# Two unused tiles that shift where the SBUF tiles of a two-block transformer kernel begin

## The chip, the cores and the metric

The kernel runs on one core of one Trainium2 chip. The metric is device time in microseconds. The kernel before took 1284.35 us (median of 3 runs, 1283.81 to 1284.84).

## The reference, cut to what matters

Two transformer blocks over 256 tokens of width 1024, all in float32. What matters here is that nearly all of the work is matrix products with weights that are read once from memory:

```
h = rms_norm(x, norm_mix);  proj = h @ w_in            # 5888 columns
att = window attention, ret = chunkwise retention of pieces of proj
merged = sigmoid(ga) * (att @ w_att_o) + sigmoid(gr) * (ret @ w_ret_o)
x = x + merged @ w_out
x = x + (silu(h @ w_gate) * (h @ w_up)) @ w_down        # 2816 hidden
x = rms_norm(x, final_norm)
proj = rms_norm(x) @ w_in_2                             # second block
x = x + concat(gated, chunk attention) @ w_out_2
# PEER: 16384 experts, 16 kept per head and token, 8 heads
q = x @ w_query;  scores = q . sub_keys;  top 16, 16x16 candidates, top 16
out[t] = sum over kept experts e of  g[t,e] * gelu(u_e . x_t) * v_e
```

The expert layer is computed densely: all 16384 rows of u against all tokens (the first layer), a table S of gates times gelu, and S against all rows of v (the second layer).

## The kernel before, in words

Activations are kept transposed, 128 partitions by (block of 128 features, 256 tokens). Every float32 operand of a large product is split in two parts of type float32r: a rounded high part (`hi`, ScalarE, line 95 or 156) and the rest (`lo`, VectorE, line 96 or 157). A product is then three matmuls that add up in PSUM: high by high, high by low, low by high (`mm3`, lines 108 to 112). The trace shows these operands as f32.

`unit` (lines 77 to 100) fetches one block of weights, 128 partitions by 1024 floats, from memory into a buffer `raw` and splits it into `whi` and `wlo`. There are four `raw` buffers and two pools of three pairs `whi`, `wlo`, one of which (`wa`) is closed before the expert layer. A scheduler orders the instructions of each engine; the loads of weights are put 80 places ahead of their uses.

There are three forms of float32r matmul, and a matmul has two operands: the moving one (`rhs`), whose columns stream through TensorE, and the stationary one (`lhsT`), which a weight load (PEld) brings in before each matmul:

- `gemm_t` and `gemm_k` (lines 117 to 129; also written out for `w_att_o`): moving 256 columns of activations (`acth`, `actl`, `hidh`, `hidl`, `att`, `xbh`, `xbl`), stationary 128 columns of `whi` or `wlo`. This is called the 256-column form here.
- `gemm_n` (lines 139 to 151): moving 512 columns of `whi` or `wlo`, stationary 128 columns of activations (`acth`, `actl`).
- `second_layer` (lines 1082 to 1088, matmul on line 1087): moving 512 columns of `whi` or `wlo` (the last six only 256), stationary 128 columns of `keys` or `q`, which hold the split S.

```
109  mm = self.nc.tensor.matmul
110  mm(ps, lhsT=left[0], rhs=right[0], start=first, stop=False)
111  mm(ps, lhsT=left[0], rhs=right[1], start=False, stop=False)
112  mm(ps, lhsT=left[1], rhs=right[0], start=False, stop=last)
```

Besides these there are some 400 plain float32 matmuls (attention, retention, transposes, sums by a column of ones on line 190, expert scores on line 906) and 256 of float16 (line 960).

SBUF is given out from two ends of each partition. Pools that are opened in the ordinary way stack up from the low addresses: `const`, `tiny`, then `xb`, `actp` (the activations), `res`, `work` and what the blocks open. Pools that are opened under `using_default_side("right")` stack down from the high addresses: first `wb` with its four `raw` and three `whi`, `wlo`, then `wa`, and in the expert layer `gs`, `query` (with `keys` and `q`) and others in its place.

Of the kernel before, what the change touches and what calls it, by code (L numbers as in the profile page):

```python
# [7 lines left out]
F32 = mybir.dt.float32  # L8
# [35 lines left out]
class Net:  # L44
# [175 lines left out]
    def run(self):  # L220
        self.wpools, self.turn = [], 0
        with self.tc.using_default_side("right"):
            self.weights("wb", self.stack, 4, 3)
        self.xbp = self.pool("xb", 1)
        with ExitStack() as st:
            actp = self.pool("actp", 2, st)
            self.res = self.pool("res", 2, st)
            self.work = self.pool("work", 2, st)
            with ExitStack() as sw:
                with self.tc.using_default_side("right"):  # L230
                    self.weights("wa", sw, 0, 3)
                x2, h, acc, acg = self.block1(actp)
                x3, h, acc = self.block2(actp, x2, h, acc, acg)
            self.wpools.pop()
            self.peer(st, x3, h, acc)
# [971 lines left out]
```

## Time and profile before

| | |
|---|---|
| median of 3 runs | 1284.35 us |
| the profiled execution's own time | 1283.83 us |
| its span, first to last instruction | 1282.0 us |
| PE busy | 1272.5 us, 99% |
| weight loads busy | 1183.7 us, 92% |
| VectorE busy | 904.6 us, 71% |
| ScalarE busy | 718.3 us, 56% |
| GpSimd busy | 269.9 us, 21% |
| mean granted TensorE clock | 0.999 of full |
| memory read and written | 240.93 and 10.55 MB |

How to read it: the span is 1.8 us shorter than the time of the execution that it belongs to, and that execution is 0.5 us below the median of the runs. A matmul's "busy" time is longer than its share of the engine, since matmuls overlap; what a matmul costs is the distance from its start to the start of the next, called its pitch here. It is read from the starts in the timeline, or from a count in a stretch in which PE is busy all the time.

### The profile page before, as it was taken

To read this page: it belongs to the slowest core of one execution; us is meant where nothing else is said; L and a number is where in the kernel's file an instruction comes from. 1 tells how busy PE (TensorE), PEld (TensorE's weight loads), DVE (VectorE), ACT (ScalarE), POOL (GpSimd) and SP (SyncE) were. 2 spreads that over 40 slices of the span, in tenths; PEclk is the share of its full clock that TensorE was granted. 3 is DMA by queue.
4 is the path that set the end of the run, shared out by engine and by line. 5 is a ranking of instruction groups with operands and counts; after the bars stand their busy time and mean duration, and the time that the engine had idled before them with its cause. 6 is when DMAs were issued, how large, how long until landed. Compare 5 with 4: busy or idle time off the path is not lost.

```text
span 1282.0 us, 23578 instructions
## 1 busy us (share of the span) xinstructions
PE 1272.5 (99%) x9128; PEld 1183.7 (92%) x9128; DVE 904.6 (71%) x1786; ACT 718.3 (56%) x1158; POOL 269.9 (21%) x173
## 2 busy tenths in 40 slices
PE   8999999999999999999999999999999999999998
PEld 8978999999999889999999999999988888888887
DVE  7867577766666877988895566676566666666665
ACT  5555455554454776655554676666455555555553
POOL 2000000000000000008777787773000000000000
PEclk9999999999999999999999999999999999999999
DMA  7735659966666445567777777777767777777764
GB/s 242 267 132 164 181 181 319 320 185 189 173 188 224 149 137 156 178 186 192 180 165 212 182 167 172 175 166 178 216 212 219 219 220 218 217 218 219 218 198 160
DMA packets 91072, 253.02 MB, mean 197 GB/s; under 512 B 26960, under 2 KB 29008, under 8 KB 90832
## 3 DMA queue, kind: packets, MB, share of 16 engines
q1 hardware_dynamic: 68960, 241.58, 61.6%
q0 software_dynamic: 20992, 8.46, 5.9%
q8 instruction: 71, 1.16, 0.4%
q10 hardware_dynamic: 1008, 1.47, 0.3%
q14 instruction: 41, 0.34, 0.1%
HBM read 240.93 MB, written 10.55 MB: 196 GB/s over the span
## 4 chain that ended last, share of the span: by engine, by line
PE 93%; DVE 5%; issue 1%; DMA 0%; ACT 0%; SPq 0%; DVEq 0%; ACTq 0%
PE ax L1087 27%; PE mm L110 21%; PE mm L111 20%; PE mm L112 20%; DVE wlo L96 2%; PE ax L960 1%; DVE itop L759 1%; PE ax L906 0%; DMA xT<-in_xT_dram 0%; DVE stop L757 0%; DVE sc L762 0%; DVE pos L759 0%; ACT whi L95 0%; PE ax L450 0%; PE ax L696 0%
## 5 line engine op out<-in xcount | busy, mean ns | idle before, releaser
L96 DVE TENSOR_TENSOR wlo<-raw,whi 128x1024 fp32r<-128x1024 f32 (+2 forms) x433 | 524.3, 1213 | 236.4 <-ACT whi L95 229.9
L95 ACT ACTIVATE whi<-raw 128x1024 fp32r<-128x1024 f32 (+3 forms) x439 | 457.8, 1045 | 314.4 <-PE mm L111 219.8
L110 PE MATMUL mm<-xbh,whi 128*128 128x256 f32 x1104 | 311.8, 282 | 0.0
L112 PE MATMUL mm<-xbh,wlo 128*128 128x256 f32 x1104 | 308.4, 279 | 0.3 <-DVE wlo L96 0.2
L111 PE MATMUL mm<-xbl,whi 128*128 128x256 f32 x1104 | 308.2, 279 | 0.2 <-DVE xbl L157 0.2
L850 POOL DMA_INDIRECT cmat<-best,pos x128 | 242.0, 1890 | 229.0 <-DVE itop L759 169.6
L110 PE MATMUL mm<-acth,whi 128*128 128x256 f32 x840 | 236.4, 282 | 1.9 <-ACT acth L254 0.8
L111 PE MATMUL mm<-actl,whi 128*128 128x256 f32 x840 | 235.1, 280 | 2.0 <-DVE actl L255 2.0
L112 PE MATMUL mm<-acth,wlo 128*128 128x256 f32 x840 | 234.2, 279 | 0.0
L112 PEld LDWEIGHTS mm<-xbh,wlo 128*128 128x128 f32 x1104 | 207.4, 188 | 1.3 <-DVE wlo L96 0.9
L111 PEld LDWEIGHTS mm<-xbl,whi 128*128 128x128 f32 x1104 | 207.6, 188 | 0.4 <-DVE xbl L157 0.4
L110 PEld LDWEIGHTS mm<-xbh,whi 128*128 128x128 f32 x1104 | 207.6, 188 | 0.2 <-ACT xbh L156 0.2
L110 PEld LDWEIGHTS mm<-acth,whi 128*128 128x128 f32 x840 | 157.8, 188 | 3.2 <-ACT acth L254 1.0
L111 PEld LDWEIGHTS mm<-actl,whi 128*128 128x128 f32 x840 | 157.9, 188 | 2.6 <-DVE actl L255 2.6
L1087 PE MATMUL ax<-whi,q 128*128 128x512 f32 x513 | 158.2, 389 | 0.0
L1087 PE MATMUL ax<-whi,keys 128*128 128x512 f32 x513 | 158.1, 389 | 0.0
L112 PEld LDWEIGHTS mm<-acth,wlo 128*128 128x128 f32 x840 | 157.9, 188 | 0.2 <-DVE wlo L96 0.2
L1087 PE MATMUL ax<-wlo,keys 128*128 128x512 f32 x513 | 158.0, 389 | 0.0
L156 ACT ACTIVATE keys<-S 128x256 fp32r<-128x256 f32 x128 | 53.4, 418 | 151.4 <-PE ax L1087 151.4
L1087 PEld LDWEIGHTS ax<-whi,q 128*128 128x128 f32 x513 | 96.3, 188 | 19.9
L1087 PEld LDWEIGHTS ax<-wlo,keys 128*128 128x128 f32 x513 | 96.3, 188 | 19.9
L1087 PEld LDWEIGHTS ax<-whi,keys 128*128 128x128 f32 x513 | 96.2, 188 | 20.0
(283 smaller groups left out, 1414.2 us busy)
## 6 DMA issues: line engine op xcount, KB each, us to landing
raw<-in_peer_u_dram SPq DMA_DIRECT2D x128, 512.0 KB
raw<-in_peer_v_dram SPq DMA_DIRECT2D x128, 512.0 KB
raw<-in_w_in_b_dram SPq DMA_DIRECT2D x32, 512.0 KB
raw<-in_w_in_a_dram SPq DMA_DIRECT2D x31, 512.0 KB
raw<-in_w_gate_dram SPq DMA_DIRECT2D x22, 512.0 KB
raw<-in_w_up_dram SPq DMA_DIRECT2D x22, 512.0 KB
raw<-in_w_out_dram SPq DMA_DIRECT2D x16, 512.0 KB
cmat<-zero SPq DMA_DIRECT2D x16, 512.0 KB
```

The source lines that it names most:

```text
L95: self.last_copy = nc.scalar.activation(hi[:, s], raw[:, s], AF.Copy).ins
L96: low = (engine or nc.vector).tensor_tensor(out=lo[:, s], in0=raw[:, s], in1=hi[:, s].bitcast(F32), op=OP.subtract)
L110: mm(ps, lhsT=left[0], rhs=right[0], start=first, stop=False)
L111: mm(ps, lhsT=left[0], rhs=right[1], start=False, stop=False)
L112: mm(ps, lhsT=left[1], rhs=right[0], start=False, stop=last)
L156: nc.scalar.activation(hi, src, AF.Copy)
L759: yield cost + 50, lambda: nc.vector.max_index(where[:, o:o + 8], top[:, o:o + 8], vals)
L850: i = nc.gpsimd.indirect_dma_start(self.cmat, bass.IndirectOffsetOnAxis(ap=ps[:, hd, 1, k:k + 1], axis=0), bs[:, hd, 1, k:k + 1], None, co ...
L960: nc.tensor.matmul(C[:, t * 128:t * 128 + 128], lhsT=A[:, t], rhs=G[i][:, t], start=i == 0, stop=i == 1)
L1087: nc.tensor.matmul(banks[tb][o // 512][:, o % 512:o % 512 + e - o], lhsT=s[left][:, ts], rhs=w[right][:, o:e], start=first, stop=end and e ...
```

## The change

A tile of 120 floats (480 bytes in each partition) is taken from the right side before the weights' pool, and a tile of 64 floats (256 bytes) from the left side before the pool `xb`. Nothing reads or writes them.

```
@@ -220,7 +220,9 @@
     def run(self):
         self.wpools, self.turn = [], 0
         with self.tc.using_default_side("right"):
+            self.pool("edge", 1).tile([128, 120], F32, name="edge")
             self.weights("wb", self.stack, 4, 3)
+        self.pool("gap", 1).tile([128, 64], F32, name="gap")
         self.xbp = self.pool("xb", 1)
         with ExitStack() as st:
```

Everything on the right thereby begins 480 bytes lower, and everything on the left from `xb` on 256 bytes higher. The rows of all five engines, with their waits, are the same in the same order as before; only addresses differ. Where the operands of the float32r matmuls begin, as the remainder of the address by 512 bytes (all blocks of one tile lie multiples of 512 bytes apart, so that each kind of operand has one remainder):

| form, matmuls | moving, before | stationary, before | both, after |
|---|---|---|---|
| 256-column form, 6528 | 256 | 480 | 0 |
| `gemm_n`, 512 columns, 384 | 480 | 256 | 0 |
| `second_layer`, 1533 of 512 columns and 6 of 256 | 480 | 480 | 0 |

Of the plain float32 matmuls, the stationary operand of line 190 goes from 256 to 0 and its moving one stays at 384; both operands of line 906 go from 480 to 0; both operands of the matmul on line 510 from 256 to 0. The `raw` buffers go from 480 to 0, `xT` and S from 256 to 0.

## Rows read from the trace of the kernel before

**Rows 1.** The page: busy time of the engines; the chain that ended last by engine

```profile
PE 1272.5 (99%) x9128; PEld 1183.7 (92%) x9128; DVE 904.6 (71%) x1786; ACT 718.3 (56%) x1158; POOL 269.9 (21%) x173
...
PE 93%; DVE 5%; issue 1%; DMA 0%; ACT 0%; SPq 0%; DVEq 0%; ACTq 0%
```

**Rows 2.** Waits of PE, longest and shortest of seven (us in total, times, longest)

```profile
PE mm L111 <- DVE actl L255: 2.0, 3, 0.8
...
PE mm L111 <- DVE xbl L157: 0.2, 1, 0.2
```

**Rows 3.** The chain that ended last, in order of time (start us, us, what)

```profile
3.06 5.13 DMA xT<-in_xT_dram
...
929.79 347.51 PE ax L1087 x1533
```

**Rows 4.** Groups of matmuls by form: line 110's, a third of each kind

```profile
L110 PE MATMUL mm<-xbh,whi 128*128 128x256 f32 x1104 | 311.8, 282 | 0.0
...
L110 PE MATMUL mm<-acth,whi 128*128 128x256 f32 x840 | 236.4, 282 | 1.9 <-ACT acth L254 0.8 <-DVE qkv L294 0.6 <-ACT whi L95 0.5
...
L110 PE MATMUL mm<-whi,acth 128*128 128x512 f32 x128 | 51.4, 401 | 0.0
...
L110 PE MATMUL mm<-hidh,whi 128*128 128x256 f32 x176 | 49.5, 281 | 0.0
...
L110 PE MATMUL mm<-att,whi 128*128 128x256 f32 x32 | 8.9, 279 | 0.0
...
L110 PE MATMUL ax<-acth,whi 128*128 128x256 f32 x24 | 6.9, 287 | 0.0
```

**Rows 5.** Two stretches: length, busy (x count) by engine, granted clock, DMA

```profile
200.00:300.00 100.00, 100.00 (x854) 100.00 (x853) 72.60 (x112) 54.55 (x85) 0.00 (x0) 1.00 0.80 268
300.00:400.00 100.00, 100.00 (x851) 100.00 (x850) 64.46 (x88) 50.45 (x75) 0.00 (x0) 1.00 0.63 185
```

**Rows 6.** Timeline of PE in `gemm_n`, first and last of eight (start us, us)

```profile
420.55 0.40 PE L111 MATMUL mm<-wlo,acth 128*128 128x512 f32 x1
...
422.18 0.40 PE L112 MATMUL mm<-whi,actl 128*128 128x512 f32 x1
```

**Rows 7.** Timeline of PE, second layer: first of six into two banks, and the next

```profile
1273.73 0.39 PE L1087 MATMUL ax<-whi,keys 128*128 128x512 f32 x1
...
1275.09 0.62 PE L1087 MATMUL ax<-whi,keys 128*128 128x512 f32 x2
```

**Rows 8.** Timeline of PE, the last five matmuls of the second layer: first, last

```profile
1277.24 0.28 PE L1087 MATMUL ax<-wlo,keys 128*128 128x256 f32 x1
...
1277.72 0.28 PE L1087 MATMUL ax<-whi,q 128*128 128x256 f32 x1
```

**Rows 9.** Timeline of PE in the retention, plain float32, 256 columns

```profile
86.08 0.59 PE L510 MATMUL ax<-rv,sr 128*128 128x256 f32 x2
86.51 0.59 PE L511 MATMUL ax<-rv,sr 128*128 128x256 f32 x2
```

**Rows 10.** Plain float32 matmuls with little streaming: lines 190 and 906, timeline and durations

```profile
414.89 0.58 PE L190 MATMUL ax<-ones,acg 128*128 128x1 f32 x4
...
L190 PE MATMUL ax<-ones,acg x4: 250/250/250, 414.9 to 415.2; 128*128 128x1 f32 x4
...
511.19 1.05 PE L906 MATMUL ax<-keys,qT 128*128 128x128 f32 x8
...
L906 PE MATMUL ax<-keys,qT 128*128 128x128 f32 x64 | 8.8, 275 | 0.0
```

**Rows 11.** Timeline of PE, 256-column form: ends of 26 pitches and of 18

```profile
154.40 0.28 PE L110 MATMUL mm<-acth,whi 128*128 128x256 f32 x1
...
157.43 0.28 PE L112 MATMUL mm<-acth,wlo 128*128 128x256 f32 x1
...
299.79 0.28 PE L110 MATMUL mm<-acth,whi 128*128 128x256 f32 x1
...
301.91 0.28 PE L110 MATMUL mm<-acth,whi 128*128 128x256 f32 x1
```

More of the change, by code (lines that the diff above doesn't have):

```diff
@@ L222, in run @@
         with self.tc.using_default_side("right"):
+            self.pool("edge", 1).tile([128, 120], F32, name="edge")
             self.weights("wb", self.stack, 4, 3)
+        self.pool("gap", 1).tile([128, 64], F32, name="gap")
         self.xbp = self.pool("xb", 1)
```

## The prediction

> **What bounds the kernel now.** I read the page first: TensorE is busy 99% of the span and the chain that ended last is 93% matmuls, 5% VectorE [rows 1]. Next the waits of PE: seven kinds, the longest 2.0 us in all [rows 2]. Nothing but TensorE's own pace sets the time from the first weights on. The clock is no part of it: the granted clock stands at 1.00 in both stretches that I use, the full level of 2.4 GHz [rows 5]. So everything hangs on the pitch, the distance from one matmul's start to the next's, and on whether an address can change it. The reader is to see three pitches:
>
> - 256-column form (moving 256, stationary 480, as remainders by 512): 854 and 851 matmuls in 100 us each, with PE busy throughout [rows 5]: 200,000 ns / 1705 = 117.3 ns.
> - `gemm_n` (480 and 256): seven pitches from 420.55 to 422.18 [rows 6]: 232.9 ns.
> - second layer (480 and 480): 347.51 us for 1533 matmuls, without a break on the chain [rows 3]: 226.7 ns.
>
> The last two differ in nothing that streams: 512 columns of the same weight tiles at the same remainder, one weight load each. Still they are 6.2 ns apart. I looked for causes other than addresses. One is PSUM: the second layer mostly alternates between two banks, `gemm_n` stays in one. But at its end the second layer also puts three in a row into one bank, twice, and these six take 1275.09 - 1273.73 = 1.36 us, 226.7 ns each [rows 7]. What is left of what I can see is where the stationary operand begins: 480 against 256. So I take it that operand addresses matter when float32r streams at full rate. That is inferred, not isolated: the neighbouring engines' work differs too.
>
> **The change part by part.** It adds no instruction and no wait, and moves none on any queue; the loads, splits and evictions cost what they did. The one load on the chain is that of `xT`, 5.13 us at the start [rows 3]; its target goes from 256 to 0, and no row shows what a target's address does to a transfer; I give it nothing, and a tenth of it either way, 0.5 us, would be lost in the measurement. All other transfers are covered by the loads that run ahead (PE's waits above); the DMA engines are busy 0.63 to 0.80 of the two stretches [rows 5], so a faster PE has room to be fed, and VectorE at 64 to 73% and ScalarE near 55% there too.
>
> What is left are three terms, one per form, and their bounds from below come from the nearest rows, though none of them streams float32r:
>
> 1. The 512-column forms. A plain float32 matmul of 256 columns takes (86.51 - 86.08)/2 = 215 ns [rows 9], to within the rounding of two starts, some 2 ns; I take 216. It streams at half the columns per time, so this is as long as 512 float32r columns at full rate (512/2.4 = 213.3 ns) would take with hardly anything around it. Floor: 216 ns. `gemm_n` stands 16.9 above it, the second layer 10.7.
> 2. The 256-column form. By streaming alone its floor would be half of that, but each matmul needs its weight load, and that has a pace of its own: the one-column matmuls of line 190 start (0.58 - 0.25)/3 = 110 ns apart, the 128-column ones of line 906 (1.05 - 0.275)/7 = 111 ns [rows 10]. Their stationary operands begin at 256 and at 480, so a weight load alone does not mind where it begins; I take 111 ns as the floor. The form stands 6.3 above it.
>
> If alignment took away all that lies above the floors: 6528 x 6.3 = 41.1 us (the counts of line 110's rows, 1104 + 840 + 176 + 32 + 24 = 2176, times three lines [rows 4]), 1533 x 10.7 = 16.4, and 3 x 128 = 384 of `gemm_n` x 16.9 = 6.5. Together 64 us, so 1283.8 - 64 = 1220 us. That is the lower end. The Trainium skill, "TensorE: Matmul & The Clock Gate", section "Back-to-back issue gap", gives N/2.4 + 2.5 ns for an isolated warm stream, 109.2 and 215.8 ns here; by that page the sum would be 76 us and the time 1208; the trace shows no float32r matmul at that pace.
>
> The other end of each term is a loss; it is the second rival below. Between them I take the share that the trace has shown for one step in addresses: going from 480/256 to 480/480 is worth 6.2 of 16.9 ns above the floor, 0.37. The change brings both operands to the start of a 512-byte block, which I count as one more such step for every form: `gemm_n`'s pitch then ends where the second layer's does after its step, at 226.7 - 0.37 x 10.7 = 222.7. Terms: 6528 x 0.37 x 6.3 = 15.2 us; 1533 x 4.0 = 6.1; 384 x (232.9 - 222.7) = 3.9. Sum 25 us. Against the profiled execution's own time, 1283.8 - 25 = 1258.8; the median of the runs lies 0.5 us above that execution, so I say 1259 us.
>
> **The rivals.**
>
> *No change, 1284 us.* The pitch may have nothing to do with where in 512 bytes an operand begins. For it: in the same form, at the same remainders, the pitch is 3.03/26 = 116.5 ns in one stretch and 2.12/18 = 117.8 in another, so something besides addresses moves it [rows 11]; and lines 190 and 906 load weights equally fast from 256 and 480 [rows 10]. Against it: the 6.2 ns between the two 512-column forms [rows 3, 6]. The Trainium skill speaks for this rival: "SBUF — State Buffer", section "Specifications (TRN2)", has lines of 16 bytes within which accesses run at full bandwidth, and all remainders before the change are multiples of 16 already; by that page the change would be worth nothing and the time 1284 us. The trace neither shows nor excludes such lines.
>
> *Slower, 1299 us.* What counts may be not where an operand begins, but where moving and stationary begin relative to each other, because the weight load for the next matmul reads SBUF while the current one streams. After the change both begin at 0, so they stand to each other as in the second layer now, where both begin at 480. For 512 columns that is the better case: `gemm_n` would go from 232.9 to 226.7 (384 x 6.2 = 2.4 us gained), the second layer would stay. For 256 columns the trace has just one place with equal remainders, the last matmuls of the kernel: 1277.72 - 1277.24 = 0.48 us over four pitches, 120.0 ns [rows 8], 2.7 above the present mix. 6528 x 2.7 = 17.6 us lost, net 15.2: 1299 us. It decides from a pitch of 117.7 ns on (117.3 + 2.4 us / 6528). Against it: four pitches at the very end of the program are few. The Trainium skill speaks against it: the TensorE page, section "Step-by-step: what each phase is for", says that weights are read through a port of their own and take nothing from the running matmul; by that page this rival falls away. The 226.7 ns of a stream whose weight loads have time to spare [rows 3] do not show such a free ride.
>
> *All of it, 1220 us*, as worked out above, counts within my forecast's sign.
>
> **How the numbers follow.** Addresses appear to matter, and the two readings of how point to opposite sides. I give 0.48 to a gain (around 1259, its own range 1220 to 1280), 0.19 to no change, 0.33 to a loss. The gain leads because both operands beginning at a block's start removes the most ways in which a read can straddle something; the loss is close behind because its price rests on the only row of the right form and relation. A measurement of this kernel can tell some 0.2%, 2.6 us, from no change; the chances are meant by that bound. The range that should hold the time 8 times in 10 goes from 1222 (just short of all floors reached) to 1301 (the second rival with a little to spare), since cases of both signs hold most of the chance.
>
> **What would show it.** In the profile after, first the pitch of the 256-column form in a full 100 us stretch: 115 (about 870 matmuls) by the forecast, 117 by no change, 120 (about 833) by the second rival, 111 (900) at the floor. Then `gemm_n`: 222.7, 232.9, 226.7, 216. Then the chain's stretch of 1533 matmuls: 341 us by the forecast, 347.5 by both rivals, 331 at the floor. The forecast is wrong in its mechanism if the second layer stays at 226.7 while `gemm_n` joins it, and wrong in its premise if none of the three pitches moves. PE should go on waiting for nothing; if it waits for `whi` or `wlo` longer than now, a gain was passed on to the splits.

## The result and the profile after

The changed kernel takes 1298.51 us (median of 4 runs, 1298.1 to 1299.91) against 1284.28 of the kernel before: a ratio of 1.0113, 95% interval 1.0098 to 1.0127. It is 14 us slower. The profiled execution has a span of 1296.3 us, 14.3 more than before.

The page after, busy time and chain, beside [rows 1]:

```profile
PE 1289.1 (99%) x9128; PEld 1203.5 (93%) x9128; DVE 905.1 (70%) x1786; ACT 718.9 (55%) x1158; POOL 268.7 (21%) x173
...
PE 98%; DVE 1%; DMA 0%; issue 0%; ACT 0%; SPq 0%; DVEq 0%
```

TensorE is busy 16.6 us longer with the same 9128 matmuls; VectorE, ScalarE and GpSimd do what they did. The chain has become more of a chain of matmuls (98% against 93%): nothing else is in the way. PE's waits are shorter than in [rows 2]; the longest kind is 1.1 us in all.

Two stretches after, beside [rows 5] (length, busy and count by engine, clock, DMA):

```profile
200.00:300.00 100.00, 100.00 (x837) 100.00 (x836) 71.00 (x111) 52.98 (x82) 0.00 (x0) 1.00 0.80 263
300.00:400.00 100.00, 100.00 (x836) 100.00 (x835) 62.98 (x85) 49.44 (x73) 0.00 (x0) 1.00 0.62 180
```

Fewer matmuls of the 256-column form fit into 100 us: 836 where there were 851, at the same granted clock of 1.00. A count takes in one or two that only reach into the stretch, so that 100 us over the count reads 0.2 to 0.3 ns low; the starts in the trace give 119.9 ns for the undisturbed pitches (those of up to 126 ns) after, and 117.1 before.

The second layer on the chain, beside [rows 3], and `gemm_n`'s timeline (first and last of fifteen), beside [rows 6]:

```profile
944.12 347.52 PE ax L1089 x1533
```

```profile
424.68 0.39 PE L111 MATMUL mm<-wlo,acth 128*128 128x512 f32 x1
...
427.85 0.39 PE L110 MATMUL mm<-whi,acth 128*128 128x512 f32 x1
```

The second layer is unchanged to 0.01 us in 347.5. `gemm_n` takes 3.17/14 = 226.4 ns in place of 232.9: it has joined the second layer. Summing the distances between starts over each form, the 256-column form goes from 777.0 to 793.5 us (+16.6), `gemm_n` from 91.1 to 89.0 (-2.0), the second layer stays at 347.5, everything else loses 0.2. Together that is 14.3 us, as much as the span has grown by.

### The profile page after: what moved, and what is told of

Same layout as the page of the kernel before. It is cut to its first block, busy times and chain, and to the rows that moved or that the text cites. A ratio compares the mean times of both kernels' runs of the same rounds, so it can differ in the third digit from the quotient of the medians.

```text
span 1296.3 us, 23578 instructions
## 1 busy us (share of the span) xinstructions
PE 1289.1 (99%) x9128; PEld 1203.5 (93%) x9128; DVE 905.1 (70%) x1786; ACT 718.9 (55%) x1158; POOL 268.7 (21%) x173
## 4 chain that ended last, share of the span: by engine, by line
PE 98%; DVE 1%; DMA 0%; issue 0%; ACT 0%; SPq 0%; DVEq 0%
PE ax L1089 27%; PE mm L110 22%; PE mm L111 22%; PE mm L112 22%; PE ax L962 1%; PE ax L908 0%; DMA xT<-in_xT_dram 0%; DVE wlo L96 0%; PE ax L698 0%; PE ax L452 0%; PE ax L733 0%; PE ax L498 0%; PE ax L486 0%; PE ax L720 0%; PE ax L511 0%
## 5 line engine op out<-in xcount | busy, mean ns | idle before, releaser
L110 PE MATMUL mm<-xbh,whi 128*128 128x256 f32 x1104 | 315.3, 286 | 0.0
L111 PE MATMUL mm<-xbl,whi 128*128 128x256 f32 x1104 | 312.1, 283 | 0.2 <-DVE xbl L157 0.2
L112 PE MATMUL mm<-xbh,wlo 128*128 128x256 f32 x1104 | 312.1, 283 | 0.0
L112 PE MATMUL mm<-acth,wlo 128*128 128x256 f32 x840 | 238.4, 284 | 0.0
L111 PEld LDWEIGHTS mm<-xbl,whi 128*128 128x128 f32 x1104 | 211.6, 192 | 0.4 <-DVE xbl L157 0.4
L110 PEld LDWEIGHTS mm<-xbh,whi 128*128 128x128 f32 x1104 | 211.6, 192 | 0.1
L112 PEld LDWEIGHTS mm<-xbh,wlo 128*128 128x128 f32 x1104 | 211.5, 192 | 0.1
L110 PEld LDWEIGHTS mm<-acth,whi 128*128 128x128 f32 x840 | 161.8, 193 | 2.2 <-ACT acth L256 1.1
L111 PEld LDWEIGHTS mm<-actl,whi 128*128 128x128 f32 x840 | 161.7, 193 | 1.4 <-DVE actl L257 1.4
L112 PEld LDWEIGHTS mm<-acth,wlo 128*128 128x128 f32 x840 | 161.7, 192 | 0.2 <-DVE wlo L96 0.2
```

## The experiments

Three theories stood at the start. **Relative**: the pitch depends on the difference of the addresses of the moving and the stationary operand, by some period. **Absolute**: to begin at a multiple of 512 is slow in itself. **Neighbours**: the pitch comes from the other engines' work and the addresses are beside the point. A difference is the moving operand's remainder minus the stationary one's, itself taken as a remainder by 512 or, where that is said, by 256.

### Both at 256, both at their old difference, one part alone

```
+            self.pool("edge", 1).tile([128, 56], F32, name="edge")     # both256: right only
+            self.pool("edge", 1).tile([128, 8], F32, name="edge")      # same_diff: right
+        self.pool("gap", 1).tile([128, 120], F32, name="gap")          #            and left
+            self.pool("edge", 1).tile([128, 120], F32, name="edge")    # edge_only: right only
```

Expected of both256: 

> Only the tile on the right, of 224 bytes, so that moving and stationary operands of all float32r matmuls begin at remainder 256: equal to each other as after the change, but not multiples of 512. Relative theory (what counts is the difference of the two remainders): as after, 256-column form 119.9 ns, gemm_n 227.7, second layer 226.7, time 1298 us. Absolute theory (beginning at a multiple of 512 is itself slow): as before, about 1284 us, 256-column form near 117.

Expected of same_diff: 

> 32 bytes on the right and 480 on the left: activations begin at 224, weights at 448, so the difference of moving and stationary (288 by 512) is as before, while every operand begins elsewhere. Relative theory: as before, 256-column form 117.1 ns, gemm_n 233, 1284 us. Absolute theory: another pitch than before, in no known direction, by several us.

Expected of edge_only: 

> One part of the change: only the 480 bytes on the right. Activations begin at 256, weights, keys and q at 0, difference 256. Relative theory: neither 1284 nor 1298 need come out, since the difference is a new one; second layer stays at 226.7 ns. If the change's loss came from the weights alone having moved to 0: 1298 us.

Measured: both256 1298.43 us, ratio 1.0114 (1.0097 to 1.0131). Nothing begins at a multiple of 512, and the kernel is as slow as the changed one. The stretch from 300 to 400 us:

```profile
300.00:400.00 100.00, 100.00 (x836) 100.00 (x835) 63.02 (x85) 49.45 (x73) 0.00 (x0) 1.00 0.62 180
```

same_diff: 1282.64 us, ratio 0.9988 (0.9978 to 0.9998). Every operand of the float32r matmuls begins elsewhere than before, the difference is the old one, and so is the time, but for a tenth of a per cent that comes back below. Its stretch:

```profile
300.00:400.00 100.00, 100.00 (x859) 100.00 (x859) 64.47 (x88) 51.00 (x75) 0.00 (x0) 1.00 0.64 186
```

edge_only: 1298.51 us, ratio 1.011 (1.0094 to 1.0127). For the relative theory I had no clear expectation here: the activations at 256, the weights at 0, a difference of 256. It is as slow as a difference of 0. That fits the relative theory if the period is 256 bytes and not 512. A beginning at a multiple of 512 is not what costs, since both256 is slow without one. But all three slow kernels (the changed one, both256, edge_only) have the weights at 0 or 256, and 1298 us is also what I had named in case the loss came from the weights alone; that weights at a multiple of 256 are slow in themselves is still open here, and the next map settles it.

### A map of pairs

The whole computation is left out; a loop runs 72 matmuls for each pair of remainders, on slices of one moving and one stationary tile.

```
+            for j in range(RUN):                    # RUN is 72
+                a, b = mo + j % (2048 // n) * n, so + j % 8 * 128
+                nc.tensor.matmul(ps[:, :n], lhsT=stat[:, b:b + 128], rhs=mov[:, a:a + n],
+                                 start=j == 0, stop=j == RUN - 1)
```

> Leaves the whole computation out; it runs 72 float32r matmuls for each of 45 pairs of remainders (moving 0 to 480 in steps of 32 with stationary 0, for 256 and for 512 columns, and six other pairs each), one after the other with nothing beside them. Relative theory: pairs with equal difference have equal pitch: (0,0), (480,480), (256,256) all 120 ns at 256 columns and 226.7 at 512; (256,480) and (224,448) as (288,0), near 117; at 512 columns (480,256) and (448,224) as (224,0), near 233. Absolute theory: pairs with equal difference differ. If the other engines' work makes the pitch: all pairs alike.

The timeline of PE in the map (start us, length of all 72 in us). The output's name tells the case: n is 256 columns and w 512, then the remainder of the moving and of the stationary operand, a for 0, b for 32 and so on to p for 480. A pitch is the length less one matmul's own 0.28 (n) or 0.39 (w), over 71.

```profile
27.14 8.80 PE L49 MATMUL naa<-mov,stat 128*128 128x256 f32 x72
35.78 8.65 PE L49 MATMUL nba<-mov,stat 128*128 128x256 f32 x72
...
95.37 8.80 PE L49 MATMUL nia<-mov,stat 128*128 128x256 f32 x72
104.00 8.65 PE L49 MATMUL nja<-mov,stat 128*128 128x256 f32 x72
...
163.59 8.56 PE L49 MATMUL nip<-mov,stat 128*128 128x256 f32 x72
171.99 8.80 PE L49 MATMUL npp<-mov,stat 128*128 128x256 f32 x72
180.62 8.79 PE L49 MATMUL nii<-mov,stat 128*128 128x256 f32 x72
189.25 8.57 PE L49 MATMUL nho<-mov,stat 128*128 128x256 f32 x72
...
214.81 16.51 PE L49 MATMUL waa<-mov,stat 128*128 128x512 f32 x72
231.16 16.97 PE L49 MATMUL wba<-mov,stat 128*128 128x512 f32 x72
247.97 16.65 PE L49 MATMUL wca<-mov,stat 128*128 128x512 f32 x72
...
482.24 16.96 PE L49 MATMUL wpi<-mov,stat 128*128 128x512 f32 x72
499.05 16.51 PE L49 MATMUL wpp<-mov,stat 128*128 128x512 f32 x72
```

With nothing beside them the matmuls repeat the kernels' pitches: (0,0), (480,480) and (256,0) take (8.80 - 0.28)/71 = 120.0 ns, (256,256) 119.9; the pair of the kernel before, (256,480), 116.6; its `gemm_n`, (480,256), 233.4, and its second layer, (480,480), 227.0. So the neighbours are out, and so is the absolute theory: weights at 480 take 120.0 ns with a moving operand at 480 and 116.6 with one at 256. The rows from a to h repeat from i to p: in steps of 32 bytes the period is 256. The eight output buffers are taken in turn, so that eight steps are also one turn of these; but (0,0), (480,480) and (256,256) fall to three different buffers and agree, while (256,480) has the buffer of (0,0) and does not. One thing did not fit: 32 by 256 is the difference of (32,0), (288,0), (256,480) and (224,448), yet the first two take 117.9 ns and the others 116.6 and 116.8.

### The other part alone, and 32 bytes

```
+        self.pool("gap", 1).tile([128, 64], F32, name="gap")           # gap_only: left only
+            self.pool("edge", 1).tile([128, 8], F32, name="edge")      # edge32: right only
```

Expected of gap_only: 

> The other part of the change alone: only the 256 bytes on the left. Activations begin at 0, weights, keys and q at 480: the difference is 32 by 512, 32 by 256, where it was 288 by 512, which is 32 by 256 too. The map of pairs repeated itself after 256 bytes, so the relative theory with a period of 256: as before, 256-column form 116.7 to 117.9 ns, gemm_n 233, 1282 to 1285 us. A relative theory with a period of 512: a new pitch. Absolute theory (activations at a multiple of 512 cost): slower than 1284.

Expected of edge32: 

> 32 bytes on the right only: activations at 256, weights, keys and q at 448, difference 64 by 256. By the map of pairs: 256-column form 117.8 ns against 117.1 before, so 6528 x 0.7 = 4.6 us slower; gemm_n at difference 192, 233.4, as before; second layer 226.7; 1288.6 us. If the map does not carry over to the whole kernel: 1284 or something else.

Measured: gap_only 1284.09 us, ratio 1.000 (0.9991 to 1.001); its difference is 32 by 256, as before the change. edge32 1288.03 us, ratio 1.0026 (1.0016 to 1.0036), 0.6 us from what the map had given; its 256-column form takes 117.75 ns by the starts. So here the map carries over to the whole kernel, and of the change's two parts the one on the right makes all of the loss.

### Narrower weight loads, steps of 4 bytes, and what came before

```
+                nc.tensor.matmul(ps[:c, :n], lhsT=stat[:, b:b + c], rhs=mov[:, a:a + n], ...
```

> Leaves the whole computation out; 72 float32r matmuls for each of 52 cases. First the weight load made narrower (128, 64, 32 stationary columns) at differences 0, 32 and 160: if moving operand and weight load are in each other's way, 512 columns fall from 227 and 233 to near 216 as the load shrinks, and 256 columns from 120 to near 109; if the moving operand's own address makes the pitch, or a fixed cost per matmul, they stay. Then differences of 4 to 28 bytes: by whole blocks of 32 bytes or finer, either all as 0 or a slope towards 32's. Then the same pairs after different predecessors: if two pitches of one pair (116.7 and 117.9 for a difference of 32) come from where the streams happen to lock, a pair changes its pitch with its predecessor; if from the addresses, (256,480) and (224,448) stay at 116.7 and (288,0) at 117.9.

Timeline of PE in the second map. The last letter is the width of the stationary operand: f for 128, h for 64, q for 32 columns; the remainders have two letters each, steps of 32 and of 4 bytes.

```profile
27.89 8.80 PE L51 MATMUL naaaaf<-mov,stat 128*128 128x256 f32 x72
36.52 8.65 PE L51 MATMUL nbaaaf<-mov,stat 128*128 128x256 f32 x72
...
53.55 8.34 PE L51 MATMUL naaaah<-mov,stat 128*64 128x256 f32 x72
61.72 8.73 PE L51 MATMUL nbaaah<-mov,stat 128*64 128x256 f32 x72
...
103.54 16.53 PE L51 MATMUL waaaaf<-mov,stat 128*128 128x512 f32 x72
...
203.42 16.84 PE L51 MATMUL waaaaq<-mov,stat 128*32 128x512 f32 x72
...
515.53 8.79 PE L51 MATMUL naaaaf<-mov,stat 128*128 128x256 f32 x72
524.16 8.65 PE L51 MATMUL njaaaf<-mov,stat 128*128 128x256 f32 x72
...
566.80 8.56 PE L51 MATMUL nhaoaf<-mov,stat 128*128 128x256 f32 x72
575.20 8.56 PE L51 MATMUL njaaaf<-mov,stat 128*128 128x256 f32 x72
```

The first question has a mixed answer. With half the weight load a difference of 0 falls from 120.0 to 113.5 ns at 256 columns, but a difference of 32 rises from 117.9 to 119.0, and at 512 columns a difference of 0 rises from 227.3 to 231.7 with a quarter of the load. So the load takes part in the pitch, or the narrower output that goes with it (64 and 32 partitions in place of 128; no run separates the two), but not as a simple thief of time: no case came near 109 or 216, as I had expected if the two operands are in each other's way. The second: steps of 4 bytes count too; in this map 4, 8, 12 and 16 bytes give 123.3, 120.0, 117.5 and 116.7 ns in the steady part (the last 24 pitches of a case, by the starts). The third explains the misfit: the same pair, (288,0), takes 117.9 ns after (0,0) and 116.6 after (224,448), 117.8 and 116.7 in the steady parts. One pair of addresses can hold two rhythms, that is lasting pitches, and which one a stream falls into depends on what ran before. This fits [rows 11], 116.5 and 117.8 ns at the same remainders, and it fits same_diff: by the starts, the kernel before has 117.8 ns from 240 to 400 us and 116.7 from 120 to 200, same_diff 116.7 in both, 859 matmuls in the stretch where the kernel before has 851. Its 256-column form takes 1.7 us less in all, which is its 0.12%.

### All differences, up and down

> Leaves the whole computation out; 48 float32r matmuls for each difference of moving and stationary from 0 to 252 bytes in steps of 4, at 256 columns, once upward and once downward, and for 512 columns in steps of 8. Relative theory with locking: each difference has one or a few pitches between 113 and 124 ns, 120.0 at 0 both ways, 116.7 or 117.8 at 32 by way of arrival, 115.6 at 248 (the pair 0 and 8 of the second map); at 512 columns 226.7 at 0 and 229 to 236 elsewhere. If the maps' values came from the order of the cases alone, the two directions would disagree widely.

The timeline of PE in this map; 48 matmuls per case, so a pitch is the length less 0.28 over 47. u is the way up, d the way down; then the difference in steps of 32 and of 4 bytes.

```profile
21.34 5.92 PE L47 MATMUL nuaa<-mov,stat 128*128 128x256 f32 x48
27.10 6.08 PE L47 MATMUL nuab<-mov,stat 128*128 128x256 f32 x48
...
182.07 5.64 PE L47 MATMUL nude<-mov,stat 128*128 128x256 f32 x48
...
296.70 5.63 PE L47 MATMUL nuga<-mov,stat 128*128 128x256 f32 x48
...
475.31 5.82 PE L47 MATMUL ndga<-mov,stat 128*128 128x256 f32 x48
...
590.32 5.64 PE L47 MATMUL ndde<-mov,stat 128*128 128x256 f32 x48
```

In the steady parts 53 of the 64 differences have the same pitch both ways to within 0.5 ns. 0 has 120.0; 4, 20, 196 and 232 are the slowest, 123.3; 32 has 116.7 both ways, so that the 117.8 of its other rhythm did not show here. The best is 112 bytes (de): 5.64 us both ways, 113.3 ns once it has settled. Two others, 144 and 192 (ga), reach 113.3 on the way up and have 118.8 and 117.8 on the way down. At 512 columns, in steps of 8, 0 is the best with 226.7 and 168 the slowest with 238.3. The value of 115.6 that I expected at 248 did not come: the fine map has 120.6 there, so what the second map showed for a stationary operand 8 bytes on is not a matter of the difference alone. A stationary operand 16 bytes on took 118.3 ns in the second map, while the same difference, 240, takes 117.2 and 117.0 here. Below steps of 32 bytes the relative theory is thus not shown; whether a single value such as 112 holds at other addresses has to be tried.

### Two versions made to gain

```
-        return (pool.tile([128, K, T], F32R, tag=tag + "h", name=tag + "h", bufs=bufs),
-                pool.tile([128, K, T], F32R, tag=tag + "l", name=tag + "l", bufs=bufs))
+        return tuple(self.shifted(pool.tile([128, K * T + 64], F32R, tag=tag + x, name=tag + x, bufs=bufs), K)
+                     for x in "hl")
+
+    def shifted(self, t, K):                                           # d112; SHIFT is 20
+        return t[:, SHIFT:SHIFT + K * T].rearrange("p (k t) -> p k t", k=K)
...
+            self.pool("edge", 1).tile([128, 40], F32, name="edge")     # d192: this line alone
```

Expected of d112 (the tile `att` is shifted in the same way): 

> A version made to gain: the activations' tiles are 256 bytes longer and their contents begin 80 bytes in, so that the difference of moving and stationary is 112 by 256 in the 256-column form, where the fine map has 113.3 ns both ways; the second layer keeps 0, gemm_n goes to 144 (233.3 in the map, as now). Relative theory: 6528 x (117.1 - 113.3) = 24.8 us less, 1259 us, 256-column form 113.3 ns. If the map's minimum does not carry over, or other work then sets the pace: between 1260 and 1284.

Expected of d192: 

> 160 bytes on the right and nothing else: difference 192 by 256 in the 256-column form, where the fine map has 113.35 ns upward and 117.76 downward, and 64 in gemm_n (228.9). If the streams lock to the slow rhythm: 117.8 ns, 6528 x 0.7 = 4.6 us lost, 384 x 4.3 = 1.7 gained, 1287 us; if to the fast one: 113.3 ns, 24.8 + 1.7 gained, 1258 us; a mixture lies between, and then the 256-column pitches must stand in two groups by stretch.

Measured: d112 1265.59 us, ratio 0.9855 (0.9838 to 0.9871); d192 1265.47 us, ratio 0.9855 (0.9839 to 0.9871). Both beat both kernels. The stretch from 200 to 300 us of d112, then of d192, beside the first line of [rows 5]:

```profile
200.00:300.00 100.00, 100.00 (x884) 100.00 (x883) 74.21 (x114) 54.98 (x83) 0.00 (x0) 1.00 0.81 269
```

```profile
200.00:300.00 100.00, 100.00 (x882) 100.00 (x881) 73.96 (x113) 53.90 (x82) 0.00 (x0) 1.00 0.81 269
```

884 and 882 matmuls where the kernel before has 854. d192 mostly fell into its fast rhythm: by the starts 5272 of its 6528 pitches are 113 or 114 ns, 977 are 117 or 118. The two groups stand by stretch, as the mixture was expected to: 113.3 ns from 240 to 400 us, 117.2 to 117.8 from 600 to 660. d112 fell 6.6 us short of what I expected. By the starts its 256-column form sums to 758.6 us against 777.0, 18.4 us less in place of 24.8. Its undisturbed pitches are 113.8 ns on average and not 113.3: the first ten after an interruption average 117.2, those from the sixteenth on 113.4, so that a stream needs some matmuls to find its rhythm. And its pitches of over 126 ns, 107 of them, sum to 28.0 us against 23.4 (91) before. Of these added 4.6 us, 0.8 lie in the first 15 us; past them PE waits longer for the splits, among others 1.2 us in four waits for `wlo` against 0.2 in one before.

## Why the prediction was wrong

What bounds the kernel was right, and with it the frame: TensorE's pace alone, three forms, no cost on any other engine, no change in the order. So was the premise that addresses count; the maps show it with nothing beside the matmuls.

The step that failed is the one between the ends, where I wrote that the change "brings both operands to the start of a 512-byte block, which I count as one more such step for every form". It is no step of that kind. I had read the 6.2 ns between 480/256 and 480/480 as a reward for a better beginning, when it was a reward for an equal one. The sign that the prediction had set for a wrong mechanism came as written: the second layer stayed at 226.7 ns while `gemm_n` joined it. both256 gives the same 1298.4 us from 256/256. Term by term: the 256-column form was to gain 15.2 us and lost 16.6; the second layer was to gain 6.1 and did not move, because its difference was 0 and stayed 0; `gemm_n` was to gain 3.9 and gained 2.0.

The second rival had the relation that counts, moving to stationary, and the price, 1299 us from 120.0 ns at the last four pitches [rows 8], with net 15.2 us lost where 14.2 came. Its reason, that the weight load reads while the matmul streams, no run isolates. I had set it behind because four pitches are few. They were few, but they were the only row of the right form and the right relation, and I weighed them against an argument with no row at all, that a block's start "removes the most ways in which a read can straddle something". The page's sentence that I set against this rival is not borne out here: the Trainium skill, "TensorE: Matmul & The Clock Gate", section "Step-by-step: what each phase is for", has the weight load take nothing from the running matmul. Here the pitch follows where the load's operand begins relative to the stream's, and the same pair goes from 120.0 to 113.5 ns with half the load and half the output. Nor does the rule for no change account for what came: the Trainium skill, "SBUF — State Buffer", section "Specifications (TRN2)", has lines of 16 bytes. Here differences that are multiples of 32 run from 113.3 to 120.0 ns.

The range held the time, since it had been carried to the second rival's price. The floors of 111 and 216 ns were seen by no run; the best in any map are 113.3 and 226.7 with a full weight load. Of the two rows behind the 111, line 906's is not one of a weight load alone: its matmuls stream 128 plain columns, which by [rows 9] come to about 108 ns themselves (an estimate, half of 215). So the two lines did not show that a weight load does not mind where it begins; line 190 does, by its one-column matmuls, which start 111 to 112 ns apart by the starts, at a remainder of 256 before and at 0 after.

What stays open is why. That the pitch depends on the difference by 256 bytes, and changes when the weight load is made narrower, fits two reads that get in each other's way; that is argued and not shown, and how they would do it was not isolated. A stream without weight loads was not tried, since each of these matmuls brings its own.

## What to carry to other kernels

Where TensorE is the bound and float32r operands stream back to back, the place of a tile in SBUF can be worth a per cent or more: here one unused tile of 160 bytes is worth 1.45%, one of 480 costs 1.1%. What counts is how moving and stationary begin relative to each other, by 256 bytes; aligning both to the same round number gave 120.0 ns at 256 columns, which none of the other multiples of 16 bytes exceeds, and 226.7 at 512 columns, the best of all. A map like the ones above takes a single run; its value has to be tried in the kernel, where the order of the matmuls and their interruptions count too (18.4 us came of the 24.8 that the map had promised). And a few matching matmuls in a trace may already hold the answer: a row of the right form outweighs an argument from tidiness.

## What the runs showed of the hardware that was not expected

- A pitch of float32r matmuls of 256 columns between 113.3 and 123.3 ns, at a granted clock of 1.00 in the maps, with no other change than where the two operands begin and what ran before.
- Two stable rhythms at one pair of addresses: 116.7 or 117.8 ns at (288,0), a difference of 32 by 256, and 113.3 or 117.8 at 192, by what ran before.
- A 512-column stream that is slower with a weight load, and an output, of 32 columns than of 128: 231.7 against 227.3 ns.
